# Rows of reciprocal roots by two transposes, and the third pair of gate and up in the other four banks

## The chip, the cores and the metric

The program runs on one core of a Trainium2 chip. The metric is device time in microseconds (us) of one execution. The engines are named as in the profile: PE is the matrix engine (TensorE), PEld its weight loads, DVE the vector engine, ACT the scalar engine, POOL the general engine (GpSimd), SP the engine that issues most of the DMAs. PSUM is the memory of eight banks (2 KB in each of 128 partitions) that the matrix engine writes its products to.

## The reference, cut to what matters

Two layers of a decoder trunk on 256 tokens of width 1024: a token mixer (block attention in layer 0, latent attention in layer 1), then an MLP with a short causal convolution in its gate. Every normalisation divides a token by the root of its mean square.

```python
def rms_norm(x, g):
    xf = x.astype(jnp.float32)
    y = xf * lax.rsqrt(jnp.mean(xf * xf, axis=-1, keepdims=True) + RMS_EPS)
    return (y * g.astype(jnp.float32)).astype(x.dtype)
...
def conv_ffn(xn, w_gate, conv_w, conv_b, w_up, w_down):
    S = xn.shape[1]
    g = xn @ w_gate
    gp = jnp.pad(g, ((0, 0), (CONV_WIDTH - 1, 0), (0, 0)))
    gc = conv_b + sum(conv_w[j] * gp[:, j:j + S] for j in range(CONV_WIDTH))
    h = jax.nn.gelu(gc, approximate=False) * (xn @ w_up)
    return h @ w_down
...
    for i in range(DEPTH):
        ...
        h = h + mix.astype(h.dtype)
        f = conv_ffn(rms_norm(h, norm_ffn[i]), ffn_w_gate[i], ffn_conv_w[i], ffn_conv_b[i], ffn_w_up[i], ffn_w_down[i])
        h = h + f.astype(h.dtype)
    return rms_norm(h, norm_final)
```

Here `DEPTH` is 2, the MLP's inner width is 2816, and all numbers are float32.

## The kernel before

The 256 tokens stay on the chip, with the model's width on the partitions (`h`, 8 blocks of 128 x 256). The weights, 100 MB in all, are read once, in 192 units of about 128 x 1024 (`load_unit`, the DMA into `raw`). Each unit is split on arrival into a high part (`whi`, a cast on ACT, L173) and the rest (`wlo`, a subtraction on DVE, L174). Every product of a weight block with an activation block is then three matmuls in the fp32r format (`mm3`, L178 to L180): high by high, low by high, high by low, 128 x 128 weights against 256 tokens.

The division by the root is put off: the products are made with the undivided activations (`zh`, `zl`) while the sum of squares is still being made, and the root is multiplied in afterwards. `SumSq.columns` (L209) brings the sums to one column per 128 tokens, `rstd` (L212) turns them into reciprocal roots `r` (128 x 2: token on the partition), and `rows` (L229) lays them along the free dimension, the same row in all 128 partitions, so that a block with the width on its partitions can be multiplied by it. `rows` is called five times: once in `first_group` of layer 0 (L613), once in each MLP through `rows_sb` (L459), and twice among the latents of layer 1 (L724 and L731).

The eight banks are two rings of four: `acc` for long accumulations, `sc` for scores, flips and other short work. `ffn` runs over 11 pairs of 128-wide blocks (`f0` = 0, 2, ... 20). Each pair takes one bank for gate (`pg`) and one for up (`pu`), and `products` fills them in two halves of 48 matmuls each. The function `gate` then reads `pg` (L438 on DVE), makes the convolution and the gelu on DVE and ACT, scales on POOL (L448), and reads `pu` (L449 on DVE). The first pair's `gate` comes late, because its roots are made only after its products: its columns (L209) stand behind the first pair's products, and `rows` behind the first half of the second pair's. So two pairs are alive when the third begins. After the gate and up products, `to_layer1` or `to_out` makes the down projection in all four `sc` banks.

The code is written as one stream. A scheduler then orders the instructions of each engine by times that it estimates, and picks of a ring the bank that it expects to be free first, so that a small edit can move instructions elsewhere.

Of the kernel before, what the change touches and what calls it, by code (L numbers as in the profile page):

```python
# [10 lines left out]
F32 = mybir.dt.float32  # L11
F32R = mybir.dt.float32r
AF = mybir.ActivationFunctionType
ALU = mybir.AluOpType
PSUM = bass.MemoryType.PSUM

P = 128
S = 256
NT = S // P
# [101 lines left out]
def trunk(ctx: ExitStack, tc: tile.TileContext, xT, scalars, gfin, wstream, consts_in, out):  # L121
    nc = tc.nc
# [3 lines left out]
    act = ctx.enter_context(tc.tile_pool(name="act", bufs=1))  # L126
    sm = ctx.enter_context(tc.tile_pool(name="sm", bufs=4))
    ps = ctx.enter_context(tc.tile_pool(name="ps", bufs=1, space=PSUM))
# [15 lines left out]
    ident = cst[:, 0:P]  # L144
# [3 lines left out]
    ones = const.tile([P, P], F32, name="ones")  # L148
# [9 lines left out]
    def load_unit(cuts=2, pieces=1, mid=None):  # L158
        u = state["u"]
        state["u"] += 1  # L160
        n = UCOLS[u]
        raw = rawp.tile([P, UW], F32, name="raw")
        hi = wp.tile([P, UW], F32R, name="whi")
        lo = wp.tile([P, UW], F32R, name="wlo")
        for i in range(pieces):
            a, b = n * i // pieces, n * (i + 1) // pieces
            src = bass.AP(tensor=wstream.tensor, offset=wstream.offset + UOFF[u] + a, ap=[[n, P], [1, b - a]])
            nc.sync.dma_start(raw[:, a:b], src)
            if mid is not None and i == 0:
                mid()  # L170
        for i in range(cuts):
            a, b = n * i // cuts, n * (i + 1) // cuts
            nc.scalar.copy(hi[:, a:b], raw[:, a:b])  # L173
            nc.vector.tensor_sub(lo[:, a:b], raw[:, a:b], hi[:, a:b].bitcast(F32))  # L174
        return hi, lo

    def mm3(o, lh, ll, rh, rl, first, last):
        nc.tensor.matmul(o, lh, rh, start=first, stop=False, skip_group_check=True)  # L178
        nc.tensor.matmul(o, ll, rh, start=False, stop=False, skip_group_check=True)  # L179
        nc.tensor.matmul(o, lh, rl, start=False, stop=last, skip_group_check=True)  # L180
# [31 lines left out]
    def rstd(pc, n):  # L212
        ms = sm.tile([P, NT], F32, name="ms")
        nc.vector.tensor_scalar(ms, pc, 1.0 / n, EPS, op0=ALU.mult, op1=ALU.add)
        r = sm.tile([P, NT], F32, name="r")
        nc.gpsimd.tensor_tensor(r, ms, mhalf.to_broadcast([P, NT]), op=ALU.pow)
        return r
# [10 lines left out]

    def rows(r):  # L229

        dg = act.tile([P, NT, P], F32, name="ssacc", bufs=2)
        nc.vector.tensor_tensor(dg, ident[:, None, :].to_broadcast([P, NT, P]),
                                r[:, :, None].to_broadcast([P, NT, P]), op=ALU.mult)
        pr = ps.tile([P, S], F32, name="sc", bufs=4)
        nc.tensor.matmul(pr, ones, dg.rearrange("p t q -> p (t q)"), start=True, stop=True)  # L235
        return pr

    def rows_sb(r):
        R = act.tile([P, S], F32, name="R", bufs=2)
        nc.scalar.copy(R, rows(r))  # L240
        return R
# [177 lines left out]
    def ffn(layer, zh, zl, ss):  # L419
        with tc.tile_pool(name=f"ff{layer}", bufs=1) as fp:  # L420
            fp.tile([P, 32], F32, name="pad")
            hh = fp.tile([P, FC, S], F32R, name="hh")
            hl = fp.tile([P, FC, S], F32R, name="hl")
            st = {}

            def products(f0, j, pg, pu):
                ug, uu = load_unit(), load_unit()
                runs = ((0, KD),) if f0 + j else ((0, KD - 2), (KD - 2, KD))
                for a, b in runs:
                    for k in range(a, b):  # L430
                        for (wh, wl), dst in ((ug, pg), (uu, pu)):
                            c = slice(k * P, (k + 1) * P)
                            mm3(dst[:, j], wh[:, c], wl[:, c], zh[:, k], zl[:, k], k == 0, k == KD - 1)

            def gate(f0, pg, pu):
                Rb = st["R"][:, None, :].to_broadcast([P, 2, S])
                gm = fp.tile([P, 2, S], F32, name="gm", bufs=2)
                nc.vector.tensor_tensor(gm, pg, Rb, op=ALU.mult)  # L438
                gc = fp.tile([P, 2, S], F32, name="gc", bufs=2)
                for j in range(2):  # L440
                    w = cv[:, layer, f0 + j]
                    nc.scalar.activation(gc[:, j], gm[:, j], AF.Identity, scale=w[:, 2:3], bias=w[:, 3:4])
                    nc.vector.scalar_tensor_tensor(gc[:, j, 1:], gm[:, j, :S - 1], w[:, 1:2], gc[:, j, 1:],
                                                   op0=ALU.mult, op1=ALU.add)
                    nc.vector.scalar_tensor_tensor(gc[:, j, 2:], gm[:, j, :S - 2], w[:, 0:1], gc[:, j, 2:],
                                                   op0=ALU.mult, op1=ALU.add)
                nc.scalar.activation(gc, gc, AF.Gelu)  # L447
                nc.gpsimd.tensor_tensor(gc, gc, Rb, op=ALU.mult)  # L448
                nc.vector.tensor_tensor(gm, pu, gc, op=ALU.mult)  # L449
                nc.scalar.copy(hh[:, f0:f0 + 2], gm)  # L450
                nc.vector.tensor_sub(hl[:, f0:f0 + 2], gm, hh[:, f0:f0 + 2].bitcast(F32))

            late = None
            for f0 in range(0, FC, 2):
                pg = ps.tile([P, 2, S], F32, name="acc", bufs=4)
                pu = ps.tile([P, 2, S], F32, name="acc", bufs=4)
                products(f0, 0, pg, pu)
                if late:
                    st["R"] = rows_sb(r)  # L459
                    gate(*late)  # L460
                    late = None
                products(f0, 1, pg, pu)
                if f0 == 0:
                    r = rstd(ss.columns(), D)
                    late = (f0, pg, pu)
                else:
                    gate(f0, pg, pu)
            (to_layer1 if layer == 0 else to_out)(fp, hh, hl)
# [89 lines left out]
    with tc.tile_pool(name="at0", bufs=1) as ap:  # L558
# [30 lines left out]
        def first_group():  # L589
# [5 lines left out]
            for k in range(KD):  # L595
                split_gain(k, GM, zh, zl)
                if k % 2 == 0:
                    qk[k // 2] = load_unit(2, 2, mid=lambda: nc.sync.dma_start(h[:, k + 1:k + 2], xT[:, k + 1:k + 2]))
                if k % 4 == 0:
                    v[k // 4] = load_unit(2, 2)  # L600
                if k % 2 and k + 1 < KD:
                    nc.sync.dma_start(h[:, k + 1:k + 2], xT[:, k + 1:k + 2])
                if k == 2:
                    nc.sync.dma_start(cst, consts_in[:, :CR0])
                for kk in (k, k + 1) if k == KD - 2 else (k,) if k < KD - 2 else ():
                    sq = ap.tile([P, S], F32, name="sq0", bufs=2)
                    nc.scalar.activation(sq, h[:, kk], AF.Square)
                    ss.add(sq)
                if k == KD - 2:
                    r = rstd(ss.columns(), D)  # L610
                    st["r"] = r
                if k == KD - 1:
                    R = rows(r)  # L613
                    nc.vector.tensor_tensor(ropeR, ropeR, R[:, None, :].to_broadcast([P, 3, S]), op=ALU.mult)
                wh, wl = qk[k // 2]
                for w in range(2):
                    for i in range(2):
                        c = slice((k % 2) * 512 + (2 * w + i) * P, (k % 2) * 512 + (2 * w + i + 1) * P)
                        mm3(pqs[w][:, i], wh[:, c], wl[:, c], zh[:, k], zl[:, k], k == 0 and i == 0, k == KD - 1)
                for t in range(NT):  # L620
                    mm_v(pv, v[k // 4], k, t, k == 0 and t == 0)
# [60 lines left out]
        finish(accs, us, [(oh[:, k], ol[:, k]) for k in (KD - 2, KD - 1)], GF, zh, zl, ss)  # L682

    ffn(0, zh, zl, ss)


    zh, zl = nxt["z"]
    with tc.tile_pool(name="at1", bufs=1) as ap:
# [17 lines left out]
        pr = ps.tile([P, S], F32, name="acc", bufs=4)  # L706
# [4 lines left out]
        r = rstd(nxt["ss"].columns(), D)  # L711
# [132 lines left out]
        finish(accs, us, [(oh[:, k], ol[:, k]) for k in (KD - 2, KD - 1)], GF + KD, zh, zl, ss)  # L844

    ffn(1, zh, zl, ss)


# [25 lines left out]
```

## Time and profile before

| | us |
|---|---|
| median of 3 runs | 598.65 |
| lowest and highest of them | 593.72 and 603.82 |
| the profiled execution | 597.3 |
| its span, first to last instruction | 595.5 |
| PE busy in the span | 581.6 |

The profiled execution is 1.8 us longer than its span, and 1.35 us under the median. The mean granted clock of PE in it is 0.995 of full speed. A row of a timeline gives the start of an instruction, its length, engine, line, operation and operands. Matmuls overlap, so what one costs PE is the distance from its start to the start of the next, not its length.

### The profile page before, as it was taken

To read this page: it belongs to the slowest core of one execution; us is meant where nothing else is said; L and a number is where in the kernel's file an instruction comes from. 1 tells how busy PE (TensorE), PEld (TensorE's weight loads), DVE (VectorE), ACT (ScalarE), POOL (GpSimd) and SP (SyncE) were. 2 spreads that over 40 slices of the span, in tenths; PEclk is the share of its full clock that TensorE was granted. 3 is DMA by queue.
4 is the path that set the end of the run, shared out by engine and by line. 5 is a ranking of instruction groups with operands and counts; after the bars stand their busy time and mean duration, and the time that the engine had idled before them with its cause. 6 is when DMAs were issued, how large, how long until landed. Compare 5 with 4: busy or idle time off the path is not lost.

```text
span 595.5 us, 12164 instructions
## 1 busy us (share of the span) xinstructions
PE 581.6 (98%) x4695; PEld 556.0 (93%) x4695; DVE 422.6 (71%) x908; ACT 356.2 (60%) x768; POOL 50.3 (8%) x47
## 2 busy tenths in 40 slices
PE   8998999999999999999999999999999999999995
PEld 7987999999999999999999888999999999988884
DVE  6898774595978788754498888667788677784503
ACT  7778687565666566543476676555756556473302
POOL 1000000001110100200002200000110101210001
PEclk9998999999999999999999999999999999999999
DMA  8768443536556656675636413346466646655101
GB/s 289 288 190 279 168 145 107 176 125 196 166 188 210 209 168 208 196 227 181 200 125 234 143 35 109 106 145 192 131 213 215 204 154 205 193 189 192 62 1 70
DMA packets 30074, 101.76 MB, mean 171 GB/s; under 512 B 3488, under 2 KB 4848, under 8 KB 30016
## 3 DMA queue, kind: packets, MB, share of 16 engines
q1 hardware_dynamic: 29744, 100.24, 52.1%
q8 instruction: 37, 0.61, 0.4%
q0 software_dynamic: 128, 0.48, 0.3%
q10 hardware_dynamic: 144, 0.26, 0.1%
q14 instruction: 21, 0.17, 0.1%
HBM read 99.92 MB, written 1.05 MB: 170 GB/s over the span
## 4 chain that ended last, share of the span: by engine, by line
PE 82%; issue 10%; ACT 3%; DMA 2%; DVE 1%; POOL 1%; SPq 0%; POOLq 0%; ACTq 0%
PE acc L178 21%; PE acc L179 21%; PE acc L180 21%; PE sc L180 3%; PE sc L179 3%; PE sc L178 3%; PE sc L279 3%; DMA raw<-in_wstream 2%; PE sc L330 2%; PE sc L316 2%; ACT whi L173 1%; PE sc L807 1%; ACT pb L296 1%; PE sc L235 0%; PE sc L209 0%
## 5 line engine op out<-in xcount | busy, mean ns | idle before, releaser
L174 DVE TENSOR_TENSOR wlo<-raw,whi 128x512 fp32r<-128x512 f32 (+1 forms) x371 | 240.2, 688 | 71.9 <-ACT whi L173 71.4
L173 ACT CAST whi<-raw 128x512 fp32r<-128x512 f32 (+1 forms) x371 | 210.1, 618 | 114.1 <-PE acc L180 53.0
L178 PE MATMUL acc<-zh,whi 128*128 128x256 f32 x880 | 248.0, 282 | 0.6 <-ACT whi L173 0.6
L179 PE MATMUL acc<-zh,wlo 128*128 128x256 f32 x880 | 245.9, 279 | 0.0
L180 PE MATMUL acc<-zl,whi 128*128 128x256 f32 x880 | 245.3, 279 | 0.0
L178 PEld LDWEIGHTS acc<-zh,whi 128*128 128x128 f32 x880 | 165.7, 189 | 2.4 <-ACT whi L173 1.1
L180 PEld LDWEIGHTS acc<-zl,whi 128*128 128x128 f32 x880 | 166.5, 189 | 0.0
L179 PEld LDWEIGHTS acc<-zh,wlo 128*128 128x128 f32 x880 | 165.4, 188 | 0.4 <-DVE wlo L174 0.2
L448 POOL TENSOR_TENSOR gc<-gc,R 128x512 f32<-128x512 f32 x22 | 34.9, 1585 | 198.1 <-ACT gc L447 186.7
L178 PE MATMUL sc<-hh,whi 128*128 128x256 f32 x176 | 48.6, 276 | 0.0
L179 PE MATMUL sc<-hh,wlo 128*128 128x256 f32 x176 | 48.6, 276 | 0.0
L180 PE MATMUL sc<-hl,whi 128*128 128x256 f32 x176 | 48.6, 276 | 0.0
L450 ACT CAST hh<-gm 128x512 fp32r<-128x512 f32 x22 | 13.7, 622 | 44.1 <-DVE gm L449 44.1
L178 PE MATMUL acc<-oh,whi 128*128 128x256 f32 x128 | 38.0, 297 | 0.0
L179 PE MATMUL acc<-oh,wlo 128*128 128x256 f32 x128 | 36.0, 281 | 0.0
L180 PE MATMUL acc<-ol,whi 128*128 128x256 f32 x128 | 35.8, 280 | 0.0
L178 PE MATMUL sc<-whi,hh 128*128 128x512 f32 x88 | 34.7, 395 | 0.0
L180 PE MATMUL sc<-wlo,hh 128*128 128x512 f32 x88 | 34.5, 392 | 0.0
L179 PE MATMUL sc<-whi,hl 128*128 128x512 f32 x88 | 34.2, 389 | 0.0
L296 ACT ACTIVATE pb<-sb,nm 128x128 f32<-128x128 f32 x64 | 28.4, 445 | 8.2 <-DVE nm L293 8.2
L178 PEld LDWEIGHTS sc<-hh,whi 128*128 128x128 f32 x176 | 33.0, 188 | 0.0
L179 PEld LDWEIGHTS sc<-hh,wlo 128*128 128x128 f32 x176 | 33.0, 188 | 0.0
(135 smaller groups left out, 813.1 us busy)
## 6 DMA issues: line engine op xcount, KB each, us to landing
raw<-in_wstream SPq DMA_DIRECT2D x175, 512.0 KB, 4.2
raw<-in_wstream SPq DMA_DIRECT2D x13, 256.0 KB, 5.0
raw<-in_wstream SPq DMA_DIRECT2D x4, 576.0 KB, 3.9
h<-in_xT SPq DMA_DIRECT2D x8, 128.0 KB, 4.6
gl<-in_gfin SPq DMA_DIRECT2D x1, 512.0 KB, 3.7
out<-hn SPq DMA_DIRECT2D x1, 512.0 KB, 2.6
ropeR<-in_consts POOLq DMA_DIRECT2D x1, 384.0 KB, 4.5
out<-hn ACTq DMA_DIRECT2D x1, 256.0 KB, 2.8
```

Of the source, the lines that this page charges most:

```text
L173: nc.scalar.copy(hi[:, a:b], raw[:, a:b])
L174: nc.vector.tensor_sub(lo[:, a:b], raw[:, a:b], hi[:, a:b].bitcast(F32))
L178: nc.tensor.matmul(o, lh, rh, start=first, stop=False, skip_group_check=True)
L179: nc.tensor.matmul(o, ll, rh, start=False, stop=False, skip_group_check=True)
L180: nc.tensor.matmul(o, lh, rl, start=False, stop=last, skip_group_check=True)
L279: nc.tensor.matmul(o[:, a:b], *qk[i], start=i == 0, stop=i == len(qk) - 1, skip_group_check=True)
L296: nc.scalar.activation(pb[:, a:b], sb[:, a:b], AF.Exp, scale=-1.0, bias=nm[:, t:t + 1], accum_out=rs[:, t:t + 1])
L316: nc.tensor.transpose(pt[:, b * P:(b + 1) * P], pb[:, b * P:(b + 1) * P], ident)
L330: nc.tensor.matmul(o[j * HD:(j + 1) * HD, t * P:], self.v(n, t), pT[j][:, a:b], start=t == 0, stop=t == NT - 1)
L448: nc.gpsimd.tensor_tensor(gc, gc, Rb, op=ALU.mult)
L450: nc.scalar.copy(hh[:, f0:f0 + 2], gm)
L807: nc.tensor.transpose(pt[:DQK, i], st[g][:, t, i], ident)
```

## The change

`rows` no longer builds a diagonal matrix from `r` and multiplies it by a matrix of ones. It copies each column of `r` across 128 columns and transposes the two 128 x 128 blocks, which puts the same row into every partition. And the third pair of each MLP (`f0` = 4) takes its two accumulators from the ring `sc` in place of `acc`; this line runs once in each of the two layers.

```diff
     def rows(r):
 
-        dg = act.tile([P, NT, P], F32, name="ssacc", bufs=2)
-        nc.vector.tensor_tensor(dg, ident[:, None, :].to_broadcast([P, NT, P]),
-                                r[:, :, None].to_broadcast([P, NT, P]), op=ALU.mult)
+        rb = act.tile([P, NT, P], F32, name="ssacc", bufs=2)
+        nc.vector.tensor_copy(rb, r[:, :, None].to_broadcast([P, NT, P]))
         pr = ps.tile([P, S], F32, name="sc", bufs=4)
-        nc.tensor.matmul(pr, ones, dg.rearrange("p t q -> p (t q)"), start=True, stop=True)
+        for t in range(NT):
+            nc.tensor.transpose(pr[:, t * P:(t + 1) * P], rb[:, t], ident)
         return pr
...
             for f0 in range(0, FC, 2):
-                pg = ps.tile([P, 2, S], F32, name="acc", bufs=4)
-                pu = ps.tile([P, 2, S], F32, name="acc", bufs=4)
+
+                pg, pu = (ps.tile([P, 2, S], F32, name="sc" if f0 == 4 else "acc", bufs=4) for _ in range(2))
                 products(f0, 0, pg, pu)
```

The order of instructions shows what became of it on the engines. A row names the line, the operation, the tile written and the tiles read; a number behind a name tells one tile of that name from another. On PE, in the MLP of layer 0, before, the product with the diagonal stands between the two halves of the second pair (`acc_1918` and `acc_1919` are its gate and up):

```order
L179 MATMUL acc_1919<-zh_1682,wlo_1930 128x256
L180 MATMUL acc_1919<-zl_1683,whi_1929 128x256
L235 MATMUL sc_1987<-ssacc_1985,ones_88 128x256
L178 MATMUL acc_1918<-zh_1682,whi_2005 128x256
L179 MATMUL acc_1918<-zh_1682,wlo_2006 128x256
```

The single float32 matmul of L235 is 256 columns wide. On PE, at the same place, now:

```order
L179 MATMUL acc_1920<-zh_1683,wlo_1931 128x256
L180 MATMUL acc_1920<-zl_1684,whi_1930 128x256
L235 MATMUL sc_1988<-cst_82,ssacc_1986 128x128 x2
L178 MATMUL acc_1919<-zh_1683,whi_2007 128x256
L179 MATMUL acc_1919<-zh_1683,wlo_2008 128x256
```

Two transposes of 128 columns stand in its place, and nothing around them has moved. On PE, at the start of the third pair in layer 0, before (`acc_2082` and `acc_2083` are its gate and up):

```order
L179 MATMUL acc_1919<-zh_1682,wlo_2014 128x256
L180 MATMUL acc_1919<-zl_1683,whi_2013 128x256
L178 MATMUL acc_2082<-zh_1682,whi_2085 128x256
L179 MATMUL acc_2082<-zh_1682,wlo_2086 128x256
L180 MATMUL acc_2082<-zl_1683,whi_2085 128x256
...
L179 MATMUL acc_2082<-zh_1682,wlo_2086 128x256
L178 MATMUL acc_2083<-zh_1682,whi_2093 128x256
L179 MATMUL acc_2083<-zh_1682,wlo_2094 128x256
L180 MATMUL acc_2083<-zl_1683,whi_2093 128x256
L180 MATMUL acc_2082<-zl_1683,whi_2085 128x256
```

The scheduler had pulled two matmuls of gate (five in a row) ahead of the first of up. On PE, at the same place, now:

```order
L179 MATMUL acc_1920<-zh_1683,wlo_2016 128x256
L180 MATMUL acc_1920<-zl_1684,whi_2015 128x256
L178 MATMUL sc_2084<-zh_1683,whi_2087 128x256
L179 MATMUL sc_2084<-zh_1683,wlo_2088 128x256
L180 MATMUL sc_2084<-zl_1684,whi_2087 128x256
L178 MATMUL sc_2085<-zh_1683,whi_2095 128x256
L179 MATMUL sc_2085<-zh_1683,wlo_2096 128x256
L180 MATMUL sc_2085<-zl_1684,whi_2095 128x256
```

Gate and up alternate three by three from the start, as in the pairs behind. On DVE, among the latents of layer 1, before, behind the first `rows` of that stage (`lo__4291` are the roots of the key and value latent) and further on around the scaling of the rotary table by the query roots (L833):

```order
L232 TENSOR_TENSOR ssacc<-cst,lo__4291 128x256
L174 TENSOR_TENSOR wlo<-raw,whi 128x576
L743 SCALAR_TENSOR_TENSOR cl<-acc,sc_in,ch 128x256
L174 TENSOR_TENSOR wlo<-raw,whi 128x512
L727 SCALAR_TENSOR_TENSOR ssacc<-acc,sc_in,R 128x256 x2
...
L833 TENSOR_SCALAR ropeR<-rope_4403,lo__4462 128x64 x2
L251 TENSOR_TENSOR rt_4479<-acc,ropeR 128x128
L253 TENSOR_TENSOR rt_4480<-acc,ropeR 128x128
```

One split of a weight half (L174) stands ahead of L727. On DVE, at the same places, now:

```order
L232 COPY ssacc<-lo__4293 128x256
L174 TENSOR_TENSOR wlo<-raw,whi 128x576
L743 SCALAR_TENSOR_TENSOR cl<-acc,sc_in,ch 128x256
L727 SCALAR_TENSOR_TENSOR ssacc<-acc,sc_in,R 128x256 x2
...
L833 TENSOR_SCALAR ropeR<-rope_4407,lo__4466 128x64 x2
L174 TENSOR_TENSOR wlo<-raw,whi 128x512
L251 TENSOR_TENSOR rt_4483<-acc,ropeR 128x128
L253 TENSOR_TENSOR rt_4484<-acc,ropeR 128x128
```

That split has gone from ahead of L727 to a place behind L833 and ahead of the rotary products of the queries (L251, L253). In the first group one split likewise moves from ahead of L614 to behind the keys, and in the attention of layer 1 some tens of instructions of PE, DVE and ACT change places with their neighbours. POOL and SP keep their order.

## Rows read from the trace of the kernel before

**Rows 1.** The page, part 1: engine, busy us, share, instructions.

```profile
PE 581.6 (98%) x4695; PEld 556.0 (93%) x4695; DVE 422.6 (71%) x908; ACT 356.2 (60%) x768; POOL 50.3 (8%) x47
```

**Rows 2.** The waits of PE: waiter, releaser: us in total, times, longest.

```profile
PE sc L316 <- issue: 2.0, 1, 2.0
PE sc L279 <- DVE kT L571: 1.9, 1, 1.9
PE sc L807 <- POOL qn L254: 0.8, 1, 0.8
```

**Rows 3.** Timeline of PE around `rows` in layer 0's MLP.

```profile
140.51 0.28 PE L180 MATMUL acc<-zl,whi 128*128 128x256 f32 x1
140.62 0.59 PE L235 MATMUL sc<-ssacc,ones 128*128 128x256 f32 x2
140.87 0.47 PE L178 MATMUL acc<-zh,whi 128*128 128x256 f32 x1
141.17 0.28 PE L179 MATMUL acc<-zh,wlo 128*128 128x256 f32 x1
```

**Rows 4.** Timeline of PE around one flip of probabilities, layer 0.

```profile
76.03 0.28 PE L180 MATMUL acc<-zl,whi 128*128 128x256 f32 x1
76.15 0.49 PE L316 MATMUL sc<-cst,pn 128*128 128x128 f32 x3
76.40 0.36 PE L178 MATMUL acc<-zh,whi 128*128 128x256 f32 x1
76.60 0.28 PE L179 MATMUL acc<-zh,wlo 128*128 128x256 f32 x1
```

**Rows 5.** Groups by line: out<-in, shapes, count | busy us, mean ns | idle before.

```profile
L232 DVE TENSOR_TENSOR ssacc<-cst,r 128x256 f32<-128x256 f32 x4 | 1.7, 424 | 2.1 <-POOL r L216 2.1
...
L738 DVE TENSOR_TENSOR kT<-pb 32x1024 f32<-32x1024 f32 x1 | 1.2, 1218 | 0.0
L740 DVE COPY kT<-kT 32x1024 f32<-32x1024 f32 x1 | 0.7, 685 | 0.0
...
L316 PE MATMUL sc<-cst,pn 128*128 128x128 f32 x96 | 15.9, 280 | 2.0 <-issue 2.0
```

**Rows 6.** Timelines at the third pair's start: DVE and PE, layer 0; PE, layer 1.

```profile
146.55 0.69 DVE L438 TENSOR_TENSOR gm<-acc,R 128x512 f32<-128x512 f32 x1 [0.75 <-PE acc L180]
...
147.18 0.28 PE L179 MATMUL acc<-zh,wlo 128*128 128x256 f32 x1
147.39 0.36 PE L178 MATMUL acc<-zh,whi 128*128 128x256 f32 x1
147.59 0.28 PE L179 MATMUL acc<-zh,wlo 128*128 128x256 f32 x1
...
424.28 0.28 PE L179 MATMUL acc<-zh,wlo 128*128 128x256 f32 x1
...
424.69 0.28 PE L179 MATMUL acc<-zh,wlo 128*128 128x256 f32 x1
```

**Rows 7.** Timeline of PE: layer 0 and layer 1 behind the third pair's start.

```profile
147.93 0.28 PE L178 MATMUL acc<-zh,whi 128*128 128x256 f32 x1
...
150.65 0.28 PE L178 MATMUL acc<-zh,whi 128*128 128x256 f32 x1
...
312.83 0.50 PE L209 MATMUL sc<-ones,ssacc 128*128 128x2 f32 x4
...
425.04 0.28 PE L178 MATMUL acc<-zh,whi 128*128 128x256 f32 x1
...
427.87 0.28 PE L178 MATMUL acc<-zh,whi 128*128 128x256 f32 x1
...
525.74 0.40 PE L178 MATMUL sc<-whi,hh 128*128 128x512 f32 x1
```

**Rows 8.** Timeline of DVE among the latents of layer 1.

```profile
320.49 0.69 DVE L174 TENSOR_TENSOR wlo<-raw,whi 128x512 fp32r<-128x512 f32 x1
321.10 0.87 DVE L727 SCALAR_TENSOR_TENSOR ssacc<-acc,sc_in,R 128x256 f32<-128x256 f32 x2
```

## The prediction

> **What bounds the kernel now.** I read the page's busy times first, then the waits of PE, then PE's timeline at the places that the change touches. The reader is to see in the first that PE is busy for 581.6 of 595.5 us [rows 1], so only what PE itself does, or waits for, can move the time. The waits tell how little there is to win: the longest are 2.0, 1.9 and 0.8 us [rows 2], the first two in the start-up stage of layer 0, where the weights come too slowly, the third among the latents of layer 1. A wait of the third pair of gate and up is not in that list at all. So the timeline has to show what each edit is worth, by distances between starts.
>
> The timeline shows one more thing, and it is larger than both edits. Long stretches of the same matmul (128 x 128 weights against 256 tokens) run at one of two paces. In layer 0, behind the third pair's start, the rows at 147.93 and 150.65 us are 24 matmuls apart: 2.72 / 24 = 0.1133 us each. In layer 1, at the same place of the program, the rows at 425.04 and 427.87 us are again 24 apart: 2.83 / 24 = 0.1179 us each [rows 7]. The granted clock, 0.995 of full speed over the whole execution, leaves no room for these 4%. Each pace then holds without a break: the fast one until the columns of layer 1 at 312.83 us, which is (312.83 - 147.93) / 0.1133 = 1455 matmuls; the slow one until the down projection at 525.74 us, which is (525.74 - 425.04) / 0.1179 = 854 matmuls [rows 7]. Pace changes sit only at interruptions of the stream: with L209, L235, and the wait of the third pair. Between `rows` and the third pair of layer 0 it is slow as well: the 51 steps from 141.17 us [rows 3] to 147.18 [rows 6] take 0.1178 us each, and layer 1 does the same there. What the pace turns on I can't see in the rows.
>
> **The roots as rows, on PE.** The product with the diagonal is two records. From the start of the last matmul ahead of it to that of the second behind it is 141.17 - 140.51 = 0.66 us [rows 3], where two plain steps at 0.1133 us would take 0.227, so it costs 0.433 us of PE. Transposes of the same shape and format stand in the flips. Three of them stretch two steps from 0.236 (2 x 0.1179) to 76.60 - 76.03 = 0.57 us [rows 4], 0.334 us for three or 0.111 each. So two cost 0.223, and a call saves 0.21 us. Five calls lie in PE's stream, with no idle time of PE around them that could swallow it: 5 x 0.21 = 1.05 us. The bounds are nothing (if a pair pays a fixed cost that three share) and 1.4 us (two for 0.15).
>
> The Trainium skill, on the page "TensorE: Matmul & The Clock Gate", section "Part 4: PE-mode transpose", speaks against this: it gives about 275 ns for one 128 x 128 transpose inside a kernel. The rows' own length of a transpose, 280 ns in the mean of 96 [rows 5], agrees with it, but is a length and not a distance in the stream. Taken as a cost, two transposes would be an estimated 0.55 us, a loss of 0.12 a call and 0.6 in all, and the sum below would be 597.5 in place of 595.9.
>
> **The roots as rows, on DVE.** The multiplication by the identity takes 424 ns and becomes a copy. Of two instructions with 1024 elements, the two-input one takes 1218 ns and the copy 685 [rows 5]; with the share that does not grow with length, (1218 - 424) / 768 = 1.03 ns per element and so 160 ns fixed, a copy of 256 comes to 160 + 256 x 0.51 = 0.29 us. That is 0.13 us a call, between nothing and 0.13. In the MLPs and the first group it is worth nothing, since the waits of PE have no line for `rows`: between the roots and the matmul that uses them lie several us of other products. If that cover were gone, each call would gain its 0.13.
>
> **The moved split.** Among the latents of layer 1 DVE is what PE waits for: the 0.8 us of L807 [rows 2]. The split taken out ahead of L727 frees 321.10 - 320.49 = 0.61 us [rows 8], and two copies add 0.26; but the same split now stands ahead of the rotary products that the wait is for, and takes 0.61 back. What is left is between a gain of 0.3 and a loss of 0.6, if DVE loses the early gain in waits of its own. I take zero. The swaps in the attention of layer 1 have PE covered on both sides, and I cost them at nothing; without that cover each would be a split's 0.6 us.
>
> **The third pair's banks.** Before, two matmuls of gate are moved up and then PE halts for up's bank, which is gate's bank of the second pair and comes free with L438 at 146.55 + 0.69 us: two steps take 147.59 - 147.18 = 0.41 us against 0.236 plain [rows 6], a loss of 0.18. In layer 1 it is 424.69 - 424.28 = 0.41, the same. So 2 x 0.18 = 0.36 us goes, between 0.3 and 0.4. Behind it nothing is late. The two banks of `sc` have been idle since the attention, and the down projection wants them only eight pairs later. Pairs four and on take the `acc` banks of the pairs two and more before them, as they do now, and now none of them halts: the 1455 steps run without a break [rows 7].
>
> **The sum,** against the profiled execution's 597.3 (span 595.5 and 1.8 around it), 1.35 under the median of the three runs: 597.3 - 1.05 - 0.36 + 0 = 595.9 us. This is with each layer's pace as it was, or with any mix of paces that comes to about the same.
>
> **The rivals.** Both edits take away the interruptions at which the pace was set: L235 becomes another thing, and the wait is gone. So each layer's pace is open from the transposes on. A step of pace is 0.1179 - 0.1133 = 0.0046 us.
>
> First, *slow in both*. The slow pace stood after L235 in both layers before, and now no wait follows that could end it. Then layer 0 pays 1455 x 0.0046 = 6.7 us and layer 1 nothing new: 595.9 + 6.7 = 602.6, slower than the 597.3 of the profile. It decides at the transposes at about 141 us: if the matmuls behind them are 0.1179 apart, the layer is lost. For it speaks that L235 gave that pace both times; against it that transposes are another interruption, with flips that are followed by either pace.
>
> Second, *fast in both*. Layer 1 wins (854 + 51) x 0.0046 = 4.2 us, and layer 0's 51 matmuls 0.2: 595.9 - 4.4 = 591.5. For it speaks that the first half of the second pair is fast in both layers, and that a shorter interruption may leave that alone.
>
> Third, *swapped*, slow in layer 0 and fast in layer 1: 595.9 + 6.7 - 4.2 = 598.4, within noise of the forecast.
>
> The runs before fit such steps: 593.72 and 603.82 are 3.6 below and 6.5 above the profiled one. That makes it likely that the pace is drawn anew in each execution, and a median then falls in the middle.
>
> On the same page of the Trainium skill, the section "Back-to-back issue gap" knows one gap only, 262 cycles for 256 columns, an estimated 109 ns at full clock. By it there would be no second pace, and the sum would be 595.9 alone; no stretch of the trace agrees, at 113 or 118 ns.
>
> Fourth, the change does not do what it says: a transpose costs as much as half a product, and the halt comes back at another bank: 597.3, the same as before.
>
> **How the numbers follow.** Paces as before, or swapped, or mixed over the runs: 0.50, at 595.9. Slow in both 0.22, at 602.6. Fast in both 0.22, at 591.5. No effect 0.04, at 597.3. Something else 0.02, such as a split that PE then waits for. The range goes from 591.0 to 603.0: the two pace rivals with some tenths for the unknown costs. About 2% is what a measurement of this kernel can tell from no change, 12 us on 598.65. Faster than 586.7 would take both fast paces and 5 us more: 0.02. Slower than 610.6 would take both slow and 8 us more: 0.02. The rest, 0.96, is no change that can be told.
>
> **What the profile after would show.** L235 with ten records of about 280 ns, and about 0.45 us across it where 0.66 stood; no gap at the start of the third pair; L232 as a copy of about 0.29 us; PE's wait for L254 near 0.8. The paces, read from 24 matmuls behind the third pair's start in each layer, should explain whatever is left between 595.9 and the measured time at 6.7 us for layer 0 and 4.2 for layer 1. I would be wrong if the time moved by more than these steps, or if the paces are as before and the time isn't within 1 us of 595.9 in the profile.

## The result, and the profile after

| | before | after |
|---|---|---|
| median, us | 601.24 (6 runs, 593.72 to 604.64) | 590.75 (6 runs, 590.39 to 591.10) |
| the profiled execution, us | 597.3 | 590.41 |
| its span, us | 595.5 | 588.6 |

The ratio is 0.990, with a 95% interval of 0.986 to 0.994. It and the ratios below leave out runs more than 1.5% above the fastest run of the same kernel, here three of before at 603.8 to 604.6; the medians keep them, and by the medians the change is worth 601.24 - 590.75 = 10.5 us. It is faster by more than the noise and by less than 2%. The time lies close to *fast in both* (591.5), 5.2 us below the forecast of 595.9 and 0.25 us below the lower end of the range. As telling as the median is the spread: 11 us before, 0.7 after.

Part 1 of the page of after, engines as in [rows 1]:

```profile
PE 575.8 (98%) x4695; PEld 550.2 (93%) x4695; DVE 421.2 (72%) x908; ACT 355.9 (60%) x768; POOL 50.6 (9%) x47
```

The number of PE's records is the same to one, 4695; PE is busy 5.8 us less, and is still what sets the end. Its waits, as in [rows 2]:

```profile
PE sc L279 <- DVE kT L571: 1.9, 1, 1.9
PE sc L154 <- DVE whi L135: 1.5, 1, 1.5
PE acc L178 <- ACT whi L173: 0.9, 2, 0.6
PE sc L807 <- POOL qn L254: 0.9, 1, 0.9
PE sc L316 <- DVE nm L293: 0.4, 1, 0.4
```

The wait for L571 is unchanged, and so is the 1.5 us for L135, which the prediction's list of the longest ("2.0, 1.9 and 0.8") leaves out. That for L254 went from 0.8 to 0.9, and the halt of 2.0 ahead of L316 is down to 0.4. The groups of `rows` (L235 and L232, one of L232's two), as in [rows 5]:

```profile
L232 DVE COPY ssacc<-r 128x256 f32<-128x256 f32 x4 | 1.2, 293 | 2.1 <-POOL r L216 2.1
L235 PE MATMUL sc<-cst,ssacc 128*128 128x128 f32 x10 | 2.0, 280 | 0.0
```

PE's timeline of after, first around `rows` in layer 0's MLP as in [rows 3], then at the third pair's start as in [rows 6], then the ends of the stretches of [rows 7] in both layers:

```profile
138.98 0.28 PE L180 MATMUL acc<-zl,whi 128*128 128x256 f32 x1
139.10 0.38 PE L235 MATMUL sc<-cst,ssacc 128*128 128x128 f32 x2
139.24 0.36 PE L178 MATMUL acc<-zh,whi 128*128 128x256 f32 x1
139.44 0.28 PE L179 MATMUL acc<-zh,wlo 128*128 128x256 f32 x1
...
144.67 0.28 PE L180 MATMUL acc<-zl,whi 128*128 128x256 f32 x1
144.79 0.28 PE L178 MATMUL sc<-zh,whi 128*128 128x256 f32 x1
144.90 0.28 PE L179 MATMUL sc<-zh,wlo 128*128 128x256 f32 x1
...
310.71 0.50 PE L209 MATMUL sc<-ones,ssacc 128*128 128x2 f32 x4
...
415.65 0.28 PE L179 MATMUL acc<-zh,wlo 128*128 128x256 f32 x1
...
518.92 0.39 PE L178 MATMUL sc<-whi,hh 128*128 128x512 f32 x1
```

The transposes take 139.44 - 138.98 = 0.46 us across, where [rows 3] have 0.66. The third pair starts in `sc` without any halt: every step around 144.79 is 0.11 or 0.12. The paces are read from a view of windows (stretch, its length, busy us and records of PE, PEld, DVE, ACT and POOL, PE's granted clock, DMA share and GB/s). Two stretches of before:

```profile
150.00:310.00 160.00, 160.00 (x1415) 160.00 (x1414) 115.95 (x206) 91.81 (x169) 16.12 (x10) 1.00 0.60 189
430.00:515.00 85.00, 85.00 (x724) 85.00 (x723) 65.22 (x116) 49.45 (x92) 12.58 (x8) 1.00 0.61 193
```

The same two of after:

```profile
150.00:310.00 160.00, 160.00 (x1414) 160.00 (x1413) 116.38 (x205) 92.48 (x171) 16.11 (x10) 1.00 0.59 193
430.00:515.00 85.00, 85.00 (x753) 85.00 (x752) 68.20 (x121) 50.68 (x93) 12.03 (x9) 1.00 0.62 206
```

Between these two executions layer 0 was fast and has stayed fast (1415 and 1414 records in 160 us). Layer 1 has turned from 724 records in 85 us to 753, 4% more, at the same granted clock of 1.00. A window also counts the one or two records that began just before it, so 85 / (724 - 2) = 0.1177 us and 85 / (753 - 2) = 0.1132 us.

**Where the 6.9 us between the two profiled executions went**, by the starts of the same instruction in both, as a running difference: at the first L330, the attention's product with the values (63.40 and 61.81), -1.59; at L235 of layer 0's MLP (140.62 and 139.10) -1.52; at the columns of layer 1 (312.83 and 310.71) -2.12; behind the next columns, those of its MLP (412.40 and 409.98), -2.42; behind its `rows` (418.28 and 415.65) -2.63; at its down projection (525.74 and 518.92) -6.82. So 4.19 of the 6.9 come between `rows` and the down projection of layer 1, which is its change of pace and 0.18 for the halt. The edits themselves, the 0.60 of layer 0 (L235, the halt, 51 steps now fast) included, make up about 1.1.

The first 1.59 hardly belong to the change. They are a matter of where the lower clock falls. Two windows of the start-up stretch of before, and the first row of PE behind its halt of 2.0 us:

```profile
45.00:52.00 7.00, 5.20 (x62) 4.65 (x62) 7.00 (x12) 5.68 (x12) 0.00 (x0) 1.00 0.95 297
53.00:60.00 7.00, 7.00 (x49) 7.00 (x48) 4.74 (x19) 7.00 (x24) 0.00 (x0) 0.76 0.71 250
...
52.81 0.52 PE L316 MATMUL sc<-cst,pn 128*128 128x128 f32 x3 [2.02 <-issue]
```

and the same of after:

```profile
45.00:52.00 7.00, 6.46 (x60) 5.79 (x61) 7.00 (x12) 5.64 (x12) 0.00 (x0) 0.76 0.80 263
53.00:60.00 7.00, 7.00 (x63) 7.00 (x62) 4.73 (x19) 7.00 (x25) 0.00 (x0) 1.00 0.72 287
...
52.80 0.52 PE L316 MATMUL sc<-cst,pn 128*128 128x128 f32 x3 [0.41 <-DVE nm L293]
```

PE halts twice here, for 1.9 us ahead of L279 (at 45.6 and 45.5 us) and then ahead of L316. In after the granted clock is low (a mean of 0.76 over 7 us) behind the first halt: for a while matmuls are 0.21 us apart, the lower of the clock's two levels (1.2 GHz), and then the upper one (2.4 GHz) is back. That costs nothing, since L316 waits until 52.8 us for DVE all the same; the slow matmuls only fill 1.6 us of its halt. In before the clock is full there and low behind the second halt, where nothing takes it up. Of the 14 profiled executions (before, after and the twelve experiments) six have the low clock behind the first halt and a second halt of only 0.3 to 0.8 us. The other eight have a second halt of 2.0 to 2.4 us, and behind it four have the low clock (before, the transposes alone, and two with small products) and four have neither. From that first row of L316 to the first L330 takes 10.6 us in the four with the clock low behind it and 9.0 us in the other ten, long halt or short. So the 1.6 us are the clock behind the second halt. They come and go from execution to execution, and all of before, after and the experiments are subject to them.

### The profile page after: what moved, and what is told of

It reads as the page before. It is cut to its first block, busy times and chain, and to the rows that moved or that the text cites. A ratio compares the mean times of both kernels' runs of the same rounds, so it can differ in the third digit from the quotient of the medians.

```text
span 588.6 us, 12160 instructions
## 1 busy us (share of the span) xinstructions
PE 575.8 (98%) x4695; PEld 550.2 (93%) x4695; DVE 421.2 (72%) x908; ACT 355.9 (60%) x768; POOL 50.6 (9%) x47
## 4 chain that ended last, share of the span: by engine, by line
PE 78%; issue 12%; DVE 4%; ACT 2%; DMA 2%; POOL 1%; SPq 0%; POOLq 0%; DVEq 0%; ACTq 0%
PE acc L178 19%; PE acc L179 19%; PE acc L180 19%; PE sc L179 5%; PE sc L178 5%; PE sc L180 5%; PE sc L279 3%; PE sc L330 2%; DVE wlo L174 2%; PE sc L316 2%; DMA raw<-in_wstream 2%; ACT whi L173 1%; PE sc L807 1%; ACT pb L296 0%; POOL r L216 0%
## 5 line engine op out<-in xcount | busy, mean ns | idle before, releaser
L174 DVE TENSOR_TENSOR wlo<-raw,whi 128x512 fp32r<-128x512 f32 (+1 forms) x371 | 239.9, 687 | 70.9 <-ACT whi L173 70.6
L178 PE MATMUL acc<-zh,whi 128*128 128x256 f32 (+1 forms) x816 | 228.1, 280 | 0.3 <-ACT whi L173 0.3
L179 PE MATMUL acc<-zh,wlo 128*128 128x256 f32 (+1 forms) x816 | 226.5, 278 | 0.2 <-DVE wlo L174 0.2
L180 PE MATMUL acc<-zl,whi 128*128 128x256 f32 (+1 forms) x816 | 226.2, 277 | 0.0
L178 PEld LDWEIGHTS acc<-zh,whi 128*128 128x128 f32 (+1 forms) x816 | 153.5, 188 | 2.2 <-ACT whi L173 1.5
L179 PEld LDWEIGHTS acc<-zh,wlo 128*128 128x128 f32 (+1 forms) x816 | 153.5, 188 | 0.4 <-DVE wlo L174 0.4
L180 PEld LDWEIGHTS acc<-zl,whi 128*128 128x128 f32 (+1 forms) x816 | 153.3, 188 | 0.0
```

## The experiments

**The theory** after the result: in before, the product with the diagonal (L235) leaves the slow pace behind it, and PE's wait for a bank at the third pair then draws a new one, in each layer and each execution. That gives four mixes and the wide spread. The transposes leave the fast pace, and without the wait nothing draws again. **The rivals:** one of the two edits does it alone; or the pace has to do with something else that the edits moved (banks, transfers), and the interruptions only mark the place.

"Job" below names kernels run on one chip beside the same runs of before. The medians of before were 599.77 in the first job (29 runs, 591.6 to 604.75), 598.91 in the second (25), 603.66 in the third (7) and 602.36 in the fourth (11). That its medians differ by this much fits its mixes. The change itself gave 590.75 us, and 590.85 on another chip.

### The transposes alone, and the banks alone (first job)

After, with the third pair back in `acc`:

```diff
-                pg, pu = (ps.tile([P, 2, S], F32, name="sc" if f0 == 4 else "acc", bufs=4) for _ in range(2))
+                pg = ps.tile([P, 2, S], F32, name="acc", bufs=4)
+                pu = ps.tile([P, 2, S], F32, name="acc", bufs=4)
```

> The changed kernel with the third pair's accumulators back in the four long-accumulation banks; the two transposes stay. Theory (a pace is kept until an interruption, and the wait for the third pair's bank, whose end depends on another engine, draws it anew): the halt of 0.18 us comes back in each layer, and the times of the runs spread over 591.1 plus nothing, 4 us (layer 1 slow), 6.7 us (layer 0 slow) or both, up to 602. Rival (the transposes alone carry the gain): all runs within 1 us of 591.2. Rival (the banks alone carry it): spread as before, 594 to 604.

Measured: 597.76, ratio 0.999 (0.994 to 1.005), in 12 runs of 591.23; 595.31, 596.45, 596.61, 596.73; 597.44, 598.08, 598.24; 602.22, 603.09, 603.65 and 603.90. PE's timeline of its profiled execution (603.90) at the third pair's start in layer 0:

```profile
147.78 0.28 PE L178 MATMUL acc<-zh,whi 128*128 128x256 f32 x1
147.89 0.28 PE L179 MATMUL acc<-zh,wlo 128*128 128x256 f32 x1
148.14 0.36 PE L178 MATMUL acc<-zh,whi 128*128 128x256 f32 x1
148.33 0.28 PE L179 MATMUL acc<-zh,wlo 128*128 128x256 f32 x1
```

The halt is back (0.25 us in place of 0.113), and the pace changes with it: 0.114 ahead of it, and 150 us with 1276 records, 0.1177 each, behind. Both layers were fast up to the halt and slow behind it in this execution, while another of the same program was 12.7 us faster. The four groups of times (591; 595 to 597; 597 to 598; 602 to 604) lie where the expectation puts the four mixes (591.1, 4 us more, 6.7 us more, up to 602). That the wait draws is read from these times; the profiles show four passes of it, one that left the fast pace (layer 0 of before) and three that left the slow one.

Before, with the third pair in `sc`:

```diff
-                pg = ps.tile([P, 2, S], F32, name="acc", bufs=4)
-                pu = ps.tile([P, 2, S], F32, name="acc", bufs=4)
+                pg, pu = (ps.tile([P, 2, S], F32, name="sc" if f0 == 4 else "acc", bufs=4) for _ in range(2))
```

> The kernel before with the third pair's accumulators moved to the other four banks; the product with the diagonal stays. Theory: the product leaves the slow pace (0.118 us a matmul) in both layers, and no wait follows that could end it: every run slow in both, about 590.8 + 1.05 for the products + 6.9 + 4.2 = 603 us, slower than the median before, with a spread under 1 us. Rival (the banks alone carry the gain): about 591.8 in all runs.

Measured: 603.95 (602.25 to 604.65 in 6 runs), ratio 1.011 (1.005 to 1.017). Its windows, to be read beside those of after:

```profile
150.00:310.00 160.00, 160.00 (x1361) 160.00 (x1360) 110.39 (x193) 85.98 (x159) 16.01 (x10) 1.00 0.58 188
430.00:515.00 85.00, 85.00 (x724) 85.00 (x723) 65.89 (x117) 50.61 (x94) 13.81 (x9) 1.00 0.57 183
```

Slow in both layers here, and by the times in every run. So neither edit gains alone: the transposes alone leave the spread, and the banks alone make the kernel slower by taking away the wait that sometimes gave the fast pace. Together they are worth 10 us. This is also *slow in both* as the prediction had it, only with the product and not with the transposes.

### The product back in one layer (first job)

After, with the diagonal and the product of before in the MLP of layer 0 alone:

```diff
-                    st["R"] = rows_sb(r)
+                    st["R"] = rows_sb(r, rows if layer else rows_product)
```

> The changed kernel with the product with the diagonal back in the MLP of layer 0 alone. Theory: layer 0 goes on at 0.118 us behind it, layer 1 at 0.113: 590.8 + 0.21 + 1506 x 0.0046 = 597.9 us. Rival (the form of the interruption costs its own time on PE and no more): 591.0.

Measured: 597.71 (597.39 to 599.23 in 10 runs). Against the 590.75 of after that is 6.96, where the forecast's prices give 6.7 for layer 0's pace and 0.21 for the product. Its windows:

```profile
150.00:310.00 160.00, 160.00 (x1361) 160.00 (x1360) 110.36 (x193) 85.97 (x159) 16.01 (x10) 1.00 0.59 188
430.00:515.00 85.00, 85.00 (x752) 85.00 (x752) 68.76 (x121) 52.53 (x97) 13.71 (x9) 1.00 0.59 188
```

One instruction of PE at 139 us turns the pace of the 171 us behind it, and the MLP of the other layer doesn't feel it. The banks and all the rest of PE's order are those of after, so the rival that they set the pace falls. Its rows at the columns of layer 1 will matter further down:

```profile
317.94 0.50 PE L209 MATMUL sc<-ones,ssacc 128*128 128x2 f32 x4
...
318.50 0.28 PE L179 MATMUL acc<-zh,wlo 128*128 128x256 f32 x1
...
321.09 0.28 PE L180 MATMUL acc<-zl,whi 128*128 128x256 f32 x1
```

The last two are 22 steps apart, 2.59 / 22 = 0.1177 us each: the columns found the slow pace here and left it slow.

### Small products in the stream (first to third job)

The columns (L209), two products of 2 columns in four records, also stood where paces change. Put without use behind the transposes in layer 1 of after:

```diff
                     st["R"] = rows_sb(r)
+                    if layer == 1:
+                        dm = ps.tile([P, NT, 2], F32, name="sc", bufs=4)
+                        for t in range(2):
+                            nc.tensor.matmul(dm[:, t], ones, ones[:, :2], start=True, stop=True)
```

> The changed kernel with two unused products of two columns (ones by ones, the form of the columns of L209) behind the transposes in the MLP of layer 1 alone. Theory: this form turned the pace wherever it stands in a long stretch, so layer 1 goes on at 0.118 us from there: 590.8 + 0.44 for the products + 4.2 = 595.4 us. Rival (an interruption costs its own time on PE and no more): 591.2.

Measured: 591.37 (591.00 to 593.88 in 10 runs), and 708 records in the 80 us from 430: fast. The theory that this form always turns the pace fell here. But the products stood right behind the transposes, 417.29 and 417.07 us, so the stream was interrupted once and not twice. The next kernel has them by themselves, ahead of the fourth pair:

```diff
+                if layer == 1 and f0 == 6:
+                    dm = ps.tile([P, NT, 2], F32, name="sc", bufs=4)
+                    for t in range(NT):
+                        nc.tensor.matmul(dm[:, t], ones, ones[:, :2], start=True, stop=True)
                 products(f0, 0, pg, pu)
```

> The changed kernel with two unused products of two columns in the MLP of layer 1, standing alone between the third and the fourth pair. In the run with them right behind the transposes the pace stayed fast, against the theory that their form turns it. Theory now (they turn it when they are the whole interruption, as the columns do): the 768 matmuls of pairs four to eleven go at 0.118 us: 590.8 + 0.44 + 3.5 = 594.7 us. Rival (the pace does not turn on them at all): 591.2.

Measured: 595.24 (594.44 to 597.14 in 10 runs). Its timeline of PE, layer 1:

```profile
432.08 0.28 PE L179 MATMUL sc<-zh,wlo 128*128 128x256 f32 x1
...
432.53 0.28 PE L180 MATMUL sc<-zl,whi 128*128 128x256 f32 x1
432.65 0.50 PE L460 MATMUL sc<-ones 128*128 128x2 f32 x4
433.01 0.36 PE L178 MATMUL acc<-zh,whi 128*128 128x256 f32 x1
433.21 0.28 PE L179 MATMUL acc<-zh,wlo 128*128 128x256 f32 x1
...
435.92 0.28 PE L178 MATMUL acc<-zh,whi 128*128 128x256 f32 x1
```

Ahead of the four records (432.53 - 432.08) / 4, about 0.113, behind them (435.92 - 433.21) / 23 = 0.1178: turned from fast to slow. The same edit in both layers of the kernel with the banks alone, where the pace there is slow:

```diff
+                if f0 == 6:
+                    dm = ps.tile([P, NT, 2], F32, name="sc", bufs=4)
+                    for t in range(NT):
+                        nc.tensor.matmul(dm[:, t], ones, ones[:, :2], start=True, stop=True)
                 products(f0, 0, pg, pu)
```

> The kernel with the banks moved and the product with the diagonal kept (603.95 us, slow in both layers), with two unused small products between the third and the fourth pair of both MLPs. Theory (they turn the pace): from there both layers are fast, (1364 + 768) x 0.0046 = 9.8 us less for 0.88 us of added work: 595.0 us; added work makes the kernel faster. Rival (an interruption costs its own time): 604.8.

Measured: 594.64 (593.59 to 596.83 in 10 runs), against 603.95 without the edit. Its windows ahead of the small products (158.12 us) and behind them, then the same in layer 1:

```profile
135.00:155.00 20.00, 20.00 (x171) 19.95 (x172) 14.29 (x26) 13.36 (x25) 4.03 (x3) 1.00 0.45 148
165.00:300.00 135.00, 135.00 (x1193) 135.00 (x1192) 93.61 (x160) 73.54 (x134) 12.46 (x8) 1.00 0.62 198
420.00:434.00 14.00, 14.00 (x121) 14.00 (x120) 10.98 (x21) 10.21 (x18) 3.44 (x2) 1.00 0.39 127
440.00:515.00 75.00, 75.00 (x664) 75.00 (x663) 59.09 (x105) 45.05 (x84) 10.40 (x7) 1.00 0.62 197
```

From 0.118 to 135 / 1191 = 0.1134 in layer 0 and 75 / 662 = 0.1133 in layer 1. Products of which nothing is used make the kernel 9.3 us faster. So the pace belongs to PE's stream and not to what is computed or loaded there, and in these three places two small products turned it over.

One small product, not two, in after at the place of layer 1:

```diff
+                if layer == 1 and f0 == 6:
+                    dm = ps.tile([P, 2], F32, name="sc", bufs=4)
+                    nc.tensor.matmul(dm, ones, ones[:, :2], start=True, stop=True)
```

> The changed kernel with one unused product of two columns in place of two between the third and the fourth pair of layer 1. If one turns the pace as two do: 590.8 + 0.22 + 3.5 = 594.5 us. If it takes two: 591.0.

Measured: 591.00 (590.68 to 591.74 in 4 runs), fast (708 records in the 80 us from 435): one left the pace at this place. And a product of 256 columns as in before, unused, ahead of the fourth pair in both layers of the kernel with the banks alone:

```diff
+                if f0 == 6:
+                    dm = ps.tile([P, S], F32, name="sc", bufs=4)
+                    nc.tensor.matmul(dm, ones, mask, start=True, stop=True)
```

> The kernel with the banks moved and the product with the diagonal kept (603.95 us), with one more unused product of the same form (256 columns, full float32) between the third and the fourth pair of both MLPs. If this form turns the pace, whichever it finds: fast from there, 603.95 + 0.87 - 9.8 = 595.0 us. If this form always leaves the slow pace: 604.8.

Measured: 603.89 (602.61 to 604.46 in 4 runs), 1149 records in the 135 us from 165 us: slow behind it as ahead of it. A product of this form did not turn the pace over; in every MLP profiled it left the slow one, from the fast pace (L235) and from the slow one (here).

### More transposes, and 512 columns (second job)

Four transposes in place of two, in layer 1 of after:

```diff
+                    if layer == 1:
+                        dm = ps.tile([P, S], F32, name="sc", bufs=4)
+                        for t in range(NT):
+                            nc.tensor.transpose(dm[:, t * P:(t + 1) * P], mask[:, :P], ident)
```

> The changed kernel with two more, unused, transposes behind the two of the MLP of layer 1, so four in a row. Theory (transposes leave the pace that they find): 590.8 + 0.22 = 591.0 us. Rival (it turns on how long the interruption is; four transposes last as long as the product with the diagonal, 0.44 us): layer 1 slow, 590.8 + 0.22 + 4.2 = 595.2.

Measured: 591.49 (590.74 to 591.92 in 4 runs), fast (709 records in the 80 us from 430). Small products just ahead of the down projection of layer 1, which runs in 512 columns:

```diff
+        dm = ps.tile([P, NT, 2], F32, name="acc", bufs=4)
+        for t in range(NT):
+            nc.tensor.matmul(dm[:, t], ones, ones[:, :2], start=True, stop=True)
         for f in range(FC - LAST):
```

> The changed kernel with the same two small products between the last pair and the down projection of layer 1, whose 264 matmuls are 512 columns wide and stood at 0.229 us in both kernels. If that stretch has two paces as well, 264 x 0.0046 = 1.2 us either way: 590.0 or 592.4. If it has one: 591.2.

Measured: 591.40 (590.71 to 593.78 in 10 runs). In the 40 us from 535 it has 177 records, and so has after: 0.23 us each. At this one place the small products left the matmuls of 512 columns as they were, so it seems that only the 256-wide stretches are at stake.

### A version that turns the pace earlier (fourth job)

In after, the stretch from the attention's end to the second pair is still slow in both layers. So small products ahead of `finish`, and the columns of the MLP, which would turn it back, taken apart with six matmuls between the two:

```diff
+        if turn:
+            dm = ps.tile([P, NT, 2], F32, name="sc", bufs=4)
+            for t in range(NT):
+                nc.tensor.matmul(dm[:, t], ones, ones[:, :2], start=True, stop=True)
         for b in range(KD // 2):
...
-                runs = ((0, KD),) if f0 + j else ((0, KD - 2), (KD - 2, KD))
+                runs = (((0, 1), (1, KD)) if mid else ((0, KD),)) if f0 + j else ((0, KD - 2), (KD - 2, KD))
...
+                    if mid and a == 0:
+                        mid()
```

> The changed kernel, with two unused small products ahead of the closing products of both attentions, which stand in the slow pace together with the first pair of the MLP (158 matmuls a layer), and with the two products of the columns in the MLPs taken apart by six matmuls, so that each stands alone and leaves the pace. Theory: both layers are fast from the turn on: 590.8 - 2 x (0.73 - 0.44) = 590.2 us. Rival (two single products six matmuls apart still turn it): both layers slow behind the columns, about 590.8 + 6.9 + 4.2 - 0.6 = 601 us.

The change itself again, on the same chip:

> The changed kernel itself, on the same chip as the run above, to set a step of a few tenths against: 590.8 us, all runs within 1 us of it.

Measured: 591.22 (590.76 to 592.35 in 6 runs), ratio 0.985 (0.980 to 0.991), and for the change itself 590.85 (590.38 to 592.09 in 6 runs), ratio 0.984 (0.979 to 0.990). No gain, no loss. PE's timeline of the first, layer 0 (L410: the new small products; L213: one column each; L238: the transposes):

```profile
116.47 0.50 PE L410 MATMUL sc<-ones 128*128 128x2 f32 x4
...
117.04 0.28 PE L179 MATMUL acc<-oh,wlo 128*128 128x256 f32 x1
...
117.72 0.28 PE L179 MATMUL acc<-oh,wlo 128*128 128x256 f32 x1
...
133.25 0.28 PE L213 MATMUL sc<-ones,ssacc 128*128 128x2 f32 x2
...
133.59 0.28 PE L179 MATMUL acc<-zh,wlo 128*128 128x256 f32 x1
...
134.06 0.28 PE L180 MATMUL acc<-zl,whi 128*128 128x256 f32 x1
134.18 0.28 PE L213 MATMUL sc<-ones,ssacc 128*128 128x2 f32 x2
...
134.53 0.28 PE L179 MATMUL acc<-zh,wlo 128*128 128x256 f32 x1
...
139.24 0.28 PE L180 MATMUL acc<-zl,whi 128*128 128x256 f32 x1
139.36 0.38 PE L238 MATMUL sc<-cst,ssacc 128*128 128x128 f32 x2
```

The first step came out as meant: behind L410 the pace is (117.72 - 117.04) / 6 = 0.113. The second did not. The very first column, by itself, turned the fast pace to slow: (134.06 - 133.59) / 4 = 0.1175. The second column left it slow, (139.24 - 134.53) / 40 = 0.1178. Behind the transposes it is fast again (1414 records in the 160 us from 140). So what the first stretch gains goes on the time of the small products themselves and on the slow steps behind the columns.

It also corrects the theory twice. One small product left the fast pace in the experiment with one, and one column turned it here, in both layers. And the transposes followed a slow stretch here, and a fast one followed them, so "they leave the pace that they find" is not enough.

## Why the prediction was right or wrong, point by point

Its forecast of 595.9 missed by 5.2 us. What came is the rival *fast in both*, which it had priced at 591.5 and given a chance of 0.22. Its 0.96 on a change of less than 2% held.

- **That PE alone counts** was right: PE's 98% stayed 98%, and 6.82 of the 6.9 us are found between the starts of its rows. The two halts in the start-up stage are not shown to be weights that come too slowly: in after both end with an instruction of DVE (L571, L293), and DVE is busy for all of the 7 us from 45 us.
- **The transposes** were right: two forecast at 0.223 us, 0.21 saved a call; measured 0.66 - 0.46 = 0.20 in layer 0's MLP and, between the rows behind the columns and behind `rows`, (418.28 - 412.40) - (415.65 - 409.98) = 0.21 in layer 1's. Between 312.83 and 412.40, with two calls, the gain is 0.30, not 0.42; 0.1 of it is the longer wait for L254. The fifth call, in the first group, can't be told from the start-up stretch.
- A row of L235 is 280 ns long, and two cost 0.46 - 2 x 0.113 = 0.23 us. The Trainium skill ("TensorE: Matmul & The Clock Gate", "Part 4: PE-mode transpose") gives about 275 ns for one in one kernel's context, next to a figure for bf16; this agrees with the length of these float32 rows and not with the cost in a full stream.
- **The copy on DVE**: 0.29 us forecast, 293 ns measured. **The moved split**: zero forecast, and the wait it feeds went from 0.8 to 0.9.
- **The third pair's banks** were right: the halt of 0.18 is gone in both layers, and no later pair halts.
- **The price of a pace step** was right: 6.7 us for layer 0 against 6.96 measured with the product back there, which holds 0.21 for the product; 4.2 for layer 1 and 0.18 for its halt against 4.19.
- **The step that failed** is the one from the spread of the runs to the chances: "likely that the pace is drawn anew in each execution, and a median then falls in the middle". The draw fits the spread of before, but it came with the third pair's wait: with the wait the times spread (the transposes alone, 591 to 604), without it they do not (the banks alone, 602 to 605; after, 590.4 to 591.1). The prediction itself says that both edits take away the interruptions at which the pace was set, and still put half of the chance on paces as before, swapped or mixed. With the wait gone a mix needed another instruction that draws, and the transposes in the MLPs did not: every profiled one left the fast pace. So *slow in both*, *fast in both* and a swap were left. Which of them, the profile of before could not settle; its one argument for fast, that the stretch ahead of `rows` is fast and a shorter interruption may leave it so, is what the profile of after shows and what the times of all its runs fit. The chance of 0.22 was no more than that argument.
- **The 1.1 us between 591.5 and the profiled 590.41** are the start-up stretch, 1.6 us, less 0.5 by which the other terms came short (0.2 of the first group's call that can't be seen, 0.12 of the latents', 0.19 of layer 1). The sum started from an execution that held a low clock there, and none of after's six runs is far enough above the lowest (0.7 us at most) to have held one at that place. The lower end of the range allowed nothing for that. That 591.5 comes as close as it does is in part luck, since the two errors have opposite signs.

What stays open: what in PE sets the pace. In the profiled MLPs each form did the same every time: the full float32 product left slow, the transposes fast, the columns together turned slow to fast. Elsewhere the same forms did otherwise. Two small products turned the pace in both directions, but not right behind two transposes, and at the start of layer 1 the columns left slow from slow (the product back in layer 0; the banks alone too). One small product left fast as it was, and one column turned it to slow. The transposes among the latents of layer 1, fast ahead of them, left 0.1178 us over 26 steps in the experiment with small products in layer 1, and a faster pace in after. So the form of an interruption does not settle the pace alone, and no rule tried here covers all of these. What is shown is which instructions set it in the MLPs of these kernels, and that the change took away both that gave the slow pace there.

## What to carry to other kernels

When a kernel's runs spread over 2% with no change of the granted clock, read the distance between like instructions in every long stretch before costing an edit: here 4% of a pace, set at one instruction, outweighed both edits several times over. Then ask of each edit not only what it saves but whether it takes away an instruction at which the pace is set or drawn; and test edits apart and together, since here one alone did nothing, the other alone lost 1%, and both won. An unused instruction at the right place is a cheap probe for such a state.

## What the runs showed of the hardware

- Streams of 128 x 128 weights against 256 columns run at 0.1133 or 0.1178 us a matmul, at a granted clock of 1.00 either way, and hold one pace for 85 to 171 us, through changes of bank, weights and transfers. The Trainium skill ("TensorE: Matmul & The Clock Gate", "Back-to-back issue gap") gives one gap for 256 columns at full clock, 262 cycles, an estimated 109 ns; no run here agrees. It gives it for a matmul by itself and says that in a stream the weight loads count too, so it speaks less plainly against a second pace than the prediction has it.
- Two unused products of 2 columns turned the pace from slow to fast in both layers (603.95 to 594.64 us) and from fast to slow in one (595.24). At another place, behind a slow stretch, the columns left slow (0.1177 us).
- A full float32 product of 256 columns costs 0.43 us in the stream, nearly four fp32r matmuls of the same width, and left the slow pace in every MLP profiled, at its own place and ahead of the fourth pair.
- The lower clock (a mean of 0.76 over 7 us) came behind PE's first halt in the start-up stage (1.9 to 2.2 us) in six of the 14 profiled executions, behind the second (2.0 to 2.4 us) in four, and in four not at all, though they have both halts. Only behind the second did it cost time, 1.6 us in before.
